# Mixer B, products of keys and queries of a chunk: from two row halves with 128 stationary columns to four quarter positions with 64

## The chip, the cores and the metric

The kernel runs on one core of a Trainium2 chip. The metric is device time in microseconds (us) of one execution, and less is better. Shown are three runs of the kernel before, and one profiled execution. The engines are called as in the profile: PE (TensorE, matmuls), PEld (its loads of the stationary operand, which overlap the matmuls), DVE (VectorE), ACT (ScalarE), POOL (GpSimd) and SP (SyncE, which issues most transfers).

## The reference, cut to what matters

One inference step of a backbone of two layers over 128 context tokens and 1024 latent tokens. The change lies in mixer B of the first layer, an RWKV-7 recurrence with 8 heads of 64, run forward and backward over the tokens:

```python
def step(S, inp):
    r_t, w_t, kk_t, a_t, k_t, v_t = inp
    sa = jnp.einsum('bhvk,bhk->bhv', S, -kk_t)
    S = (S * w_t[:, :, None, :] + sa[..., None] * (kk_t * a_t)[:, :, None, :]
         + v_t[..., None] * k_t[:, :, None, :])
    return S, jnp.einsum('bhvk,bhk->bhv', S, r_t)
```

The kernel computes it by chunks of 64 tokens. Inside a chunk the steps become products: each of the two kinds of keys of the chunk (`k`, and `kk * a`) with each of the two kinds of queries (`kk` and `r`), all of them scaled by the decay. These are four 64x64 tables for each chunk, head and direction. They are masked to a triangle, the `kk` part is inverted by substitution, and a short serial scan carries the state from chunk to chunk.

## The kernel before, in words

The program has four parts one after the other: the input projection and mixer A, mixer B, the output projection of layer one, and all of layer two. Tokens lie in tiles of 128; matmuls are in float32 or in a split float32r.

Mixer B works through nine items. Eight of them are a pair of heads with half of the latent tokens, the ninth takes the context tokens of all four pairs. An item holds, for each direction `d`, four tiles `x` of 128 tokens, each of two chunks `a` of 64. On the partitions lie the two heads of the pair, head `h` on partitions 64h to 64h+63 (`half_of(h)`).

For each item these generators run, and `timeline` mixes those of different items by a table of start and end times (`TIMES`); a scheduler then sets the final order on each engine from priorities and dependences:

- `b_prep` makes the scaled keys `kbt` (four slots of 64 tokens for each tile: of the first chunk the `k` keys and the `kk*a` keys, then those of the second chunk) and the scaled queries `zr` (DVE and ACT, with matmuls L949).
- `b_front` transposes keys, values and queries (L1024, copied out by ACT at L1025 to L1027), then forms the tables in `pa` (L1034). One group of L1034 is two tiles, both chunks and both heads. DVE masks `pa` into `za` (L1040) and `q` (L1042). L1049 makes a first correction of the values from `za`.
- `b_subst` and `b_invert` invert (POOL at L1067 to L1083, then PE at L1108, L1115, L1129 and L1143).
- `b_scan` carries the state: L1186, a DVE addition L1188, L1190, a DVE addition L1197, a scaling on ACT L1199; L1203 and L1163 make the outputs. It is a serial chain of eight steps for each item.
- `b_finish` normalises and gates (L1223 to L1253).

PE also works at the modulation of later layers (L298) in this part.

Every matmul of this part has float32 operands, and each appears in the trace as two records with a weight load each. The array can be used by halves: the partitions of the operands choose the rows of the array, the partitions of the output choose the columns. At L1034 before, the stationary operand is `kbt[s, x, 2a:2a+2]`, 64 partitions by 128 columns (both kinds of keys), and the moving one 64 partitions by 128 columns (both kinds of queries). So a matmul takes one half of the rows and all columns; the two heads take the two halves in turn. L1129 (`b_invert`) already uses a quarter at a time, in this order of rows and columns:

```python
for h, e in ((0, 0), (1, 1), (0, 1), (1, 0)):
    PE.matmul(pe[half_of(h), e, d, x], it.zn[half_of(e), d, x, half_of(h)],
              Rt[half_of(e), 8 * d + 2 * x + h], start=True, stop=True)
```

L1143 takes only two of the four quarters in turn, (0, 0) and (1, 1), and L1049 takes (0, 1) and (1, 0). In the trace a shape like "64*128 64x128" means a stationary operand of 64 partitions by 128 columns and a moving one of 64 by 128.

Of the kernel before, what the change touches and what calls it, by code (L numbers as in the profile page):

```python
# [141 lines left out]
def hybrid_step(ctx: ExitStack, tc: tile.TileContext, I, O, stop=99):  # L142
    nc = tc.nc
    PE, VE, AE, GE, SP = nc.tensor, nc.vector, nc.scalar, nc.gpsimd, nc.sync
# [12 lines left out]
    def tl(pool, shape, tag, dt=F32, bufs=None):  # L157
        uid[0] += 1
        kw = {} if bufs is None else {"bufs": bufs}
        return pool.tile(list(shape), dt, tag=tag, name=f"{tag}_{uid[0]}", **kw)  # L160
# [749 lines left out]
    half_of = lambda j: slice(64 * j, 64 * j + 64)  # L910
# [3 lines left out]
    def part_of(it, d):  # L914
        a = 0 if it.nl > 1 else it.start[d] - P
        return slice(a, a + 512)
# [81 lines left out]
    def b_front(it, d, pool, pre, ps_y, ps_a, vmask):  # L998

        r, v, ke, kbt = it.front[d]  # L1000
        if d == 0:
            it.q, it.kb = {}, {}
            it.VU = tl(it.pool, [P, 4, 2, 2, P], "VU")
            it.zn, it.av = tl(pre, [P, 2, 4, P], "zn", bufs=2), tl(pre, [P, 2, 4, P], "av", bufs=2)
            it.za = tl(pre, [P, 2, 2, 4, 2, 64], "za", bufs=2)
            it.kbs = tl(dp, [2, P, 512 if it.nl > 1 else 1024], "kbs", bufs=2) if it.first else it.prev.kbs
        it.q[d] = tl(it.pool, [P, 8, 2, 64], f"q{d}")
        it.kb[d] = tl(it.pool, [P, 8, P], f"kb{d}")
        order = lambda x: it.chunks(x, d)
        zr = it.zr[d]  # L1010
        kd = hb(pool, [P, 512])
        for i, p in enumerate(it.pairs):
            w = slice(None) if it.nl == 1 else slice(i, i + 1)
            VE.scalar_tensor_tensor(order(kd)[:, w], four(ke)[:, w], rkh[:, p:p + 1], order(r)[:, w], op0=ALU.mult,
                                    op1=ALU.mult)
        SP.dma_start(it.kbs[d][:, part_of(it, d)], kd)
        yield
        for x0 in (0, 2):
            for x in (x0, x0 + 1):
                pn = tl(ps_y, [P, 4, P], "py")  # L1020
                for i, src in enumerate((kbt[:, x, 0:2].rearrange("p a t -> p (a t)"),
                                         kbt[:, x, 2:4].rearrange("p a t -> p (a t)"), v[:, P * x:P * x + P],
                                         zr[:, x, 0].rearrange("p a t -> p (a t)"))):
                    PE.transpose(pn[:, i], src, ident)  # L1024
                AE.copy(it.kb[d][:, 2 * x:2 * x + 2], pn[:, 0:2])  # L1025
                AE.copy(it.VU[:, x, d], pn[:, 2:3].to_broadcast([P, 2, P]))
                AE.copy(it.zn[:, d, x], pn[:, 3])  # L1027
                yield
            pa = tl(ps_a, [P, 2, 2, 2, 2, 64], "pa")
            for x in (x0, x0 + 1):  # L1030
                for a in range(2):
                    for h in range(2):
                        s = half_of(h)
                        PE.matmul(pa[:, h, x - x0, a], kbt[s, x, 2 * a:2 * a + 2].rearrange("p a t -> p (a t)"),  # L1034
                                  zr[s, x, :, 1 - a], start=True, stop=True)
            yield
            mk = lambda i, n: vmask[:, 64 * i:64 * i + 64].rearrange("p (a b m) -> p a b m", a=1, b=1).to_broadcast(
                [P, 2, n, 64])
            for a in range(2):
                VE.tensor_tensor(it.za[:, a, d, x0:x0 + 2].rearrange("p x h t -> p h x t"), pa[:, :, :, a, 0], mk(0, 2),  # L1040
                                 ALU.mult)
            it.tail = VE.tensor_tensor(it.q[d][:, 2 * x0:2 * x0 + 4].rearrange("p c h t -> p h c t"),  # L1042
                             pa.rearrange("p h x a z t -> p h (x a) z t")[:, :, :, 1], mk(1, 4), ALU.mult)
            yield
        pv = tl(ps_y, [P, 4, 2, 64], "py")
        for x in range(4):
            for h in range(2):
                for a in range(2):
                    PE.matmul(pv[half_of(1 - a), x, h], it.za[half_of(a), a, d, x, h],  # L1049
                              it.VU[half_of(a), x, d, a, half_of(h)], start=True, stop=True)  # L1050
        AE.copy(it.av[:, d], pv.rearrange("p x h v -> p x (h v)"))
        yield
# [219 lines left out]
    with ExitStack() as ph2:  # L1272
# [28 lines left out]
        for p in range(4):  # L1301
            a = Item([p], (P, P + 512), last=False)
# [27 lines left out]
        def front(i, d):  # L1330
            return b_front(items[i], d, pool, pre, ps_y, ps_a, ma) if i < len(items) else None
# [37 lines left out]
        for i in range(-2, len(items)):  # L1369
# [47 lines left out]
            t = TIMES[min(i + 2, 2) if i < 5 else 3]  # L1417
# [470 lines left out]
```

## Time and profile before

| | before |
|---|---|
| three runs | 2088.42, 2087.62, 2074.43 us; median 2087.62 |
| profiled execution | a span of 2077.4 us from the first to the last instruction; the page gives no time outside the span, and the median of the runs is 10.2 us more |
| busy over the span | PE 1952.1 us (94%), PEld 1777.4 (86%), DVE 1488.3 (72%), ACT 1058.8 (51%), POOL 673.6 (32%) |
| L1034 | 576 records between 557.9 and 942.1 us |
| the items' front and scan stage | about 557 to 960 us of the span |

A matmul record has its start and a modelled end: records overlap, and the busy time of a group holds the fill of the array as well as its stream. What a run of matmuls takes of PE is therefore read from starts: from a group's first start to its last (its length in the timeline less the length of one record), and from there to the next group's start. The view of waits gives to each idle stretch of an engine what ended it.

### The profile page before, as it was taken

To read this page: it belongs to the slowest core of one execution; us is meant where nothing else is said; L and a number is where in the kernel's file an instruction comes from. 1 tells how busy PE (TensorE), PEld (TensorE's weight loads), DVE (VectorE), ACT (ScalarE), POOL (GpSimd) and SP (SyncE) were. 2 spreads that over 40 slices of the span, in tenths; PEclk is the share of its full clock that TensorE was granted. 3 is DMA by queue.
4 is the path that set the end of the run, shared out by engine and by line. 5 is a ranking of instruction groups with operands and counts; after the bars stand their busy time and mean duration, and the time that the engine had idled before them with its cause. 6 is when DMAs were issued, how large, how long until landed. Compare 5 with 4: busy or idle time off the path is not lost. (4 is left out here: it accounts for less than half of the span.)

```text
span 2077.4 us, 40804 instructions
## 1 busy us (share of the span) xinstructions
PE 1952.1 (94%) x15148; PEld 1777.4 (86%) x15148; DVE 1488.3 (72%) x3821; ACT 1058.8 (51%) x2808; POOL 673.6 (32%) x951
## 2 busy tenths in 40 slices
PE   7899999999789999999989999999999999999998
PEld 7899999999678888777768888999998989898786
DVE  5355567565767787877488587878787878787867
ACT  4343345333446555564356554565555555555643
POOL 0222232332167657575043223121312121212204
PEclk9999999999999999999999999999999999999999
DMA  7511133112555454534576401010101010101325
GB/s 290 163 62 65 61 98 115 63 57 78 181 178 158 146 171 148 157 111 129 167 228 218 133 21 45 15 50 10 51 9 55 6 56 5 55 5 49 106 68 177
DMA packets 165079, 205.72 MB, mean 99 GB/s; under 512 B 16368, under 2 KB 108048, under 8 KB 164880
## 3 DMA queue, kind: packets, MB, share of 16 engines
q1 hardware_dynamic: 162016, 198.25, 30.1%
q10 hardware_dynamic: 2864, 4.85, 0.7%
q8 instruction: 120, 1.97, 0.4%
q14 instruction: 79, 0.65, 0.1%
HBM read 152.32 MB, written 50.74 MB: 98 GB/s over the span
## 5 line engine op out<-in xcount | busy, mean ns | idle before, releaser
L1562 ACT ACTIVATE p<-s,mx 128x384 f32<-128x384 f32 (+1 forms) x400 | 225.1, 572 | 123.0 <-DVE mx L1559 100.3
L1557 DVE TENSOR_REDUCE mc<-s 128x1 f32<-128x384 f32 x384 | 204.4, 551 | 29.3 <-PE s L1555 26.2
L1555 PE MATMUL s<-kst,qs 128*128 128x384 f32 x768 | 196.0, 355 | 14.1 <-ACT p L1562 13.6
L360 PE MATMUL ps<-wch,hh 128*128 128x384 f32 x576 | 205.5, 358 | 3.0 <-DMA raw<-in_wgc_dram 0.9
L361 PE MATMUL ps<-wcl,hh 128*128 128x384 f32 x576 | 198.6, 345 | 4.1 <-POOL wcl L271 4.1
L362 PE MATMUL ps<-wch,hl 128*128 128x384 f32 x576 | 196.4, 341 | 0.3 <-DVE hl L1707 0.2
L407 POOL TENSOR_TENSOR q<-ropea,ropeb 128x256 f32<-128x256 f32 x56 | 44.0, 786 | 442.4 <-DVE ropeb L404 302.3
L374 PE MATMUL ps<-hh,wgh 128*128 128x384 f32 x504 | 174.5, 346 | 5.8 <-DVE bo L242 4.3
L376 PE MATMUL ps<-hh,wgl 128*128 128x384 f32 x504 | 172.4, 342 | 0.0
L375 PE MATMUL ps<-hl,wgh 128*128 128x384 f32 x504 | 171.9, 341 | 0.0
L1555 PEld LDWEIGHTS s<-kst,qs 128*128 128x128 f32 x768 | 127.5, 190 | 29.8 <-ACT p L1562 22.4
L271 POOL TENSOR_TENSOR wgl<-raw,wgh 128x1024 fp32r<-128x1024 f32 (+1 forms) x39 | 75.5, 1939 | 234.5 <-ACT wgh L270 234.5
L1083 POOL TENSOR_TENSOR rp<-rp,tmp 128x126 f32<-128x126 f32 (+22 forms) x279 | 130.3, 467 | 21.9
L1081 POOL TENSOR_TENSOR tmp<-mp,rp 128x126 f32<-128x126 f32 (+22 forms) x279 | 117.8, 422 | 52.3 <-DVE mp L1072 31.1
L1438 ACT CAST ah<-pt 128x512 fp32r<-128x512 f32 (+2 forms) x168 | 86.1, 533 | 79.7 <-PE pt L1593 76.3
L1439 DVE TENSOR_TENSOR al<-pt,ah 128x512 fp32r<-128x512 f32 (+2 forms) x168 | 100.6, 615 | 32.1 <-ACT ah L1438 30.8
L360 PEld LDWEIGHTS ps<-wch,hh 128*128 128x128 f32 x576 | 109.6, 191 | 6.5 <-DVE vl L1439 2.4
L361 PEld LDWEIGHTS ps<-wcl,hh 128*128 128x128 f32 x576 | 109.8, 191 | 6.2 <-POOL wcl L271 5.8
L362 PEld LDWEIGHTS ps<-wch,hl 128*128 128x128 f32 x576 | 109.5, 190 | 1.4 <-DVE hl L1707 1.3
L271 POOL TENSOR_TENSOR wcl<-raw,wch 128x512 fp32r<-128x512 f32 x54 | 76.5, 1423 | 84.5 <-ACT wch L270 84.5
L374 PEld LDWEIGHTS ps<-hh,wgh 128*128 128x128 f32 x504 | 95.4, 189 | 8.1 <-DVE bo L242 4.9
L1575 DVE SCALAR_TENSOR_TENSOR p<-p,lr,p 128x1152 f32<-128x1152 f32 (+1 forms) x72 | 98.4, 1367 | 0.4
(463 smaller groups left out, 5721.7 us busy)
## 6 DMA issues: line engine op xcount, KB each, us to landing
hb<-pbT SPq DMA_DIRECT2D x90, 256.0 KB, 3.9
adaw<-in_ada_w_dram SPq DMA_DIRECT2D x56, 256.0 KB, 3.6
raw<-in_wc_dram SPq DMA_DIRECT2D x48, 256.0 KB, 2.7
adaw<-in_ada_w_dram SPq DMA_DIRECT2D x8, 1024.0 KB, 10.9
pbT<-bm SPq DMA_DIRECT2D x16, 512.0 KB, 2.7
low<-lowT SPq DMA_DIRECT2D x16, 512.0 KB, 4.1
raw<-in_wo_dram SPq DMA_DIRECT2D x32, 256.0 KB, 2.8
raw<-in_wpb_dram SPq DMA_DIRECT2D x13, 512.0 KB, 3.4
```

The costliest lines, as they stand in the source:

```text
L271: eng.tensor_tensor(lo[:, j:j + w], raw[:, :w], hi[:, j:j + w].bitcast(F32), ALU.subtract)
L360: PE.matmul(ps[:, :n], hh[:, k, s], wh[:, k], start=k == 0, stop=False)
L361: PE.matmul(ps[:, :n], hh[:, k, s], wl[:, k], start=False, stop=False)
L362: PE.matmul(ps[:, :n], hl[:, k, s], wh[:, k], start=False, stop=k == KT - 1)
L374: PE.matmul(ps[:, :THIRD], wh[:, k], hh[:, k, s], start=k == 0, stop=False)
L375: PE.matmul(ps[:, :THIRD], wh[:, k], hl[:, k, s], start=False, stop=False)
L376: PE.matmul(ps[:, :THIRD], wl[:, k], hh[:, k, s], start=False, stop=k == KT - 1)
L1081: eng.tensor_tensor(tv, m[:, j - a:j - a + 1, 0:j].to_broadcast([P, n, j]), rpb[:, t:16, j:j + 1].to_broadcast([P, n, j]), ALU.mult)
L1083: eng.tensor_tensor(rpb[:, t:16, 0:j], rpb[:, t:16, 0:j], tv, ALU.add)
L1555: PE.matmul(s[c][:, :w], qs[:, e, z], hd.kp[:, z] if own else hd.kst[:, z, w * c:w * c + w], start=e == 0, stop=e == 1)
L1557: VE.tensor_reduce(mc[:, c:c + 1] if nb > 1 else mx, s[c][:, :w], axis=AX.X, op=ALU.min)
L1562: AE.activation(e[:, w * c:w * c + w], s[c][:, :w], AF.Exp, scale=-1.0, bias=mx, accum_out=sums[:, z, c:c + 1])
```

## The change

In `b_front`, the 128 stationary columns of each product are cut into two halves `e` of 64, one for each kind of keys. Half `e` goes to the columns whose outputs are partitions 64e to 64e+63 of `pa`, where the same numbers stood before. There are now four matmuls for each tile and chunk in place of two, in the order (0,0), (1,1), (0,1), (1,0) of head and half. The moving operand stays 64 by 128, and is now streamed once for each half. What is written to `pa`, and all that reads it, is the same.

```diff
@@ -1029,10 +1029,10 @@
             pa = tl(ps_a, [P, 2, 2, 2, 2, 64], "pa")
             for x in (x0, x0 + 1):
                 for a in range(2):
-                    for h in range(2):
+                    for h, e in ((0, 0), (1, 1), (0, 1), (1, 0)):
                         s = half_of(h)
-                        PE.matmul(pa[:, h, x - x0, a], kbt[s, x, 2 * a:2 * a + 2].rearrange("p a t -> p (a t)"),
-                                  zr[s, x, :, 1 - a], start=True, stop=True)
+                        PE.matmul(pa[half_of(e), h, x - x0, a], kbt[s, x, 2 * a + e], zr[s, x, :, 1 - a],
+                                  start=True, stop=True)
             yield
```

In the whole program 288 matmuls of L1034 become 576. The scheduler's order moves a little with it, only in the mixer B part; POOL's order is unchanged. On PE the 288 matmuls stood in 53 unbroken runs, 26 of them whole groups of eight; the 576 stand in 58 runs, 25 of them whole groups of sixteen.

The first place is on PE, in an item whose scan (L1186, L1190, L1203) is mixed with the products of a later item. `pa` is the table, `zr` and `kbt` are queries and keys, `sc` and `yb` belong to the scan. Before:

```order
L949 MATMUL py_6804<-low_6791,lora_6793 128x512 x2
L1034 MATMUL pa_6818<-zr_1211_6637,kbt_6640 128x128 x2
L1186 MATMUL sc_6763<-G_991_5695,E_6646 128x128 x2
L1034 MATMUL pa_6818<-zr_1211_6637,kbt_6640 128x128 x2
L1203 MATMUL yb_6727<-zr_1009_5745,S_995_5699 128x64
L1034 MATMUL pa_6818<-zr_1211_6637,kbt_6640 128x128
L1190 MATMUL sc_6763<-VU_5813,kb_1032_5819 128x128
L1190 MATMUL sc_6763<-VU_5813,kb_1046_5911 128x128
L1203 MATMUL yb_6727<-zr_1035_5831,S_995_5699 128x64
L1034 MATMUL pa_6818<-zr_1211_6637,kbt_6640 128x128 x3
```

The same place in the changed kernel:

```order
L1034 MATMUL pa_6882<-zr_1211_6701,kbt_6704 64x128
L1190 MATMUL sc_6792<-VU_5813,kb_1032_5819 128x128
L1190 MATMUL sc_6792<-VU_5813,kb_1046_5927 128x128
L949 MATMUL py_6868<-low_6855,lora_6857 128x512 x2
L1034 MATMUL pa_6882<-zr_1211_6701,kbt_6704 64x128 x4
L1186 MATMUL sc_6827<-G_991_5695,E_6710 128x128 x2
L1034 MATMUL pa_6882<-zr_1211_6701,kbt_6704 64x128 x4
L1203 MATMUL yb_6791<-zr_1009_5745,S_995_5699 128x64
L1203 MATMUL yb_6791<-zr_1035_5831,S_995_5699 128x64
L1190 MATMUL sc_6827<-VU_5813,kb_1032_5819 128x128
L1190 MATMUL sc_6827<-VU_5813,kb_1046_5927 128x128
L1034 MATMUL pa_6882<-zr_1211_6701,kbt_6704 64x128 x7
```

The group of eight stood in runs of 2, 2, 1 and 3 and now stands in runs of 1, 4, 4 and 7 of sixteen; one run starts ahead of the scan's L1190, and the two L1203 stand together.

The second place is on DVE, in one of two items where the same rows change places: the scan's additions L1188 (`VU`) and L1197 (`G`) among the work for later items (L1014) and for the output of an earlier one (L1226). Before:

```order
L1042 TENSOR_TENSOR q_1469_8140<-pa_8252,cstones_5690 128x2x4x64
L990 TENSOR_TENSOR kbt_8249<-hb_8265,hb_8191 128x4x2x64
L1188 TENSOR_TENSOR VU_6753<-VU_6753,sc_8294 64x2x128
L1014 SCALAR_TENSOR_TENSOR hb_8367<-hb_8265,rkh_5649,hb_8181 128x512
L1226 TENSOR_TENSOR hb_8270<-hb_8270,hb_8271 128x512
L1197 TENSOR_TENSOR G_992_5696<-S_993_5697,sc_8294 64x2x64 x2
L307 TENSOR_SCALAR gs_5_69<-py_8285,prm_60 128x2
```

The same place in the changed kernel:

```order
L1042 TENSOR_TENSOR q_1469_8268<-pa_8388,cstones_5690 128x2x4x64
L990 TENSOR_TENSOR kbt_8385<-hb_8409,hb_8319 128x4x2x64
L1014 SCALAR_TENSOR_TENSOR hb_8511<-hb_8409,rkh_5649,hb_8309 128x512
L1226 TENSOR_TENSOR hb_8414<-hb_8414,hb_8415 128x512
L1188 TENSOR_TENSOR VU_6817<-VU_6817,sc_8438 64x2x128
L307 TENSOR_SCALAR gs_5_69<-py_8429,prm_60 128x2
L1197 TENSOR_TENSOR G_992_5696<-S_993_5697,sc_8438 64x2x64 x2
```

L1188 moved behind L1014 and L1226, and L1197 behind L307.

## Prediction

> **What bounds the kernel now.** I read the page first, for the engine that is busy most, then busy times of the stretch in which L1034 runs, then the groups of PE in that stretch.
>
> ```profile
> span 2077.4 us, 40804 instructions
> PE 1952.1 (94%) x15148; PEld 1777.4 (86%) x15148; DVE 1488.3 (72%) x3821; ACT 1058.8 (51%) x2808; POOL 673.6 (32%) x951
> ```
>
> PE is busy 94% of the span. The stretch of the change is 557 to 960 us, here as the sum of five equal parts of it (403 us), with the columns of the view's own head:
>
> ```profile
> core 0: us, PE busy (x) PEld busy (x) DVE busy (x) ACT busy (x) POOL busy (x), PEclk, DMA share, GB/s
> sum 403.00, PE 363.25 PEld 314.20 DVE 309.41 ACT 226.81 POOL 256.11; mean PE 72.65 PEld 62.84 DVE 61.88 ACT 45.36 POOL 51.22
> ```
>
> PE is at 363 of 403 us (90%), DVE at 309 (77%). So PE, in its fixed order, is the nearest thing to a bound, and I count what L1034 takes of PE as lying on the path. The groups of PE in this stretch (busy us, mean ns of one, idle before):
>
> ```profile
> L298 PE MATMUL py<-prm,adaw 128*128 128x128 f32 x442 | 64.5, 295 | 1.8 <-DMA adaw<-in_ada_w_dram 1.6
> L1034 PE MATMUL pa<-zr,kbt 64*128 64x128 f32 x576 | 49.6, 296 | 2.3 <-DVE q L1042 1.5 <-DVE kbt L990 0.8
> L1190 PE MATMUL sc<-VU,kb 128*128 128x128 f32 x224 | 37.6, 290 | 8.8 <-DVE VU L1188 8.6
> ```
>
> L1034 covers 49.6 us, 2.4% of the span. To make the kernel faster by 1% (21 us) the change would have to take away over two fifths of that. The scan's L1190 waits 8.6 us for L1188; who waits on L1034's side is this:
>
> ```profile
> PEld pa L1034 <- issue: 8.9, 26, 1.7
> DVE za L1040 <- PE pa L1034: 10.0, 7, 3.9
> ```
>
> The chain that ended last is no help here: as the profile shows it, it reaches back only some tens of us from the end, into layer two.
>
> **What a group of L1034 costs.** A record has one length (min, median, max in ns):
>
> ```profile
> L1034 PE MATMUL pa<-zr,kbt x576: 271/272/579, 557.9 to 942.1; 64*128 64x128 f32 x192
> L1129 PE MATMUL pa<-Rt,zn x576: 218/218/312, 623.0 to 1035.6; 64*64 64x64 f32 x192
> L1143 PE MATMUL sc<-av,Rt x576: 218/218/332, 623.2 to 1037.5; 64*64 64x64 f32 x192
> ```
>
> Length of a group less one record is the time from its first to its last start. Whole and broken groups in the timeline (start, length):
>
> ```profile
> 605.45 0.27 PE L1024 MATMUL py<-cst,zr 128*128 128x128 f32 x1
> 605.65 1.16 PE L1034 MATMUL pa<-zr,kbt 64*128 64x128 f32 x16
> 606.80 1.02 PE L298 MATMUL py<-prm,adaw 128*128 128x128 f32 x7
> ...
> 629.74 0.49 PE L1034 MATMUL pa<-zr,kbt 64*128 64x128 f32 x4
> 630.16 0.71 PE L1186 MATMUL sc<-G,E 128*128 128x128 f32 x4
> ...
> 633.04 0.71 PE L1034 MATMUL pa<-zr,kbt 64*128 64x128 f32 x6
> 633.68 0.44 PE L1024 MATMUL py<-cst,kbt 128*128 128x128 f32 x2
> ...
> 636.32 0.48 PE L1034 MATMUL pa<-zr,kbt 64*128 64x128 f32 x2
> ```
>
> One product (x2): 0.48 - 0.27 = 0.21 us from its first record to its second. Two (x4): 0.22. So the two row halves run side by side. Three (x6): 0.44, as four would, since the odd one takes its rounds alone. Eight (x16): 0.89. Each further pair of products costs (0.89 - 0.22) / 3 = 0.223 us, two rounds of 0.1115. A round is the time in which every position in use starts one record. The first round is longer by 0.10: the first load of 128 columns has nothing to hide it. Entering from a 128-row matmul takes 605.65 - 605.45 = 0.20 and leaving 630.16 - (629.74 + 0.22) = 0.20; from one such matmul to the next it is 0.11.
>
> **What four positions cost.** The changed kernel's form is not in this trace, 64 columns with 128 moving. Its two neighbours are, with 64 moving columns: L1129 in four positions, L1143 in two.
>
> ```profile
> 1034.70 1.16 PE L1129 MATMUL pa<-Rt,zn 64*64 64x64 f32 x64
> 1035.69 2.03 PE L1143 MATMUL sc<-av,Rt 64*64 64x64 f32 x64
> ...
> 708.80 0.33 PE L1129 MATMUL pa<-Rt,zn 64*64 64x64 f32 x2
> ```
>
> L1143 makes 64 records in 32 rounds: (2.03 - 0.22) / 31 = 0.058 a round. L1129 makes them in 16 rounds: 1.16 - 0.22 = 0.94, which is 0.11 for the first (from the x2 row, 0.33 - 0.22) and 0.83 / 14 = 0.059 for each after it. So going from two to four positions left the round as it was. And 0.1115 is nearly twice 0.058, as 128 moving columns are twice 64. Forecast for the new form: a round of 0.1115 with four positions, and a first round of 0.11 + 0.05 = 0.16, with half the load of before. Four starts are some 0.02 apart in all (64 records of L1129: 0.94 - 0.11 - 14 x 0.058 = 0.02).
>
> There are 36 groups (9 items, 2 directions, 2 halves). A whole group before is 8 products in 2 positions, 8 rounds. After, it is 16 products in 4 positions: 8 rounds again. **The array was full before**, two halves by 128 columns; it is full after, four quarters. Twice the records at twice the rate is the same time.
>
> **The sum.** In PE's order there are 53 runs of L1034 before. Two products share two rounds, an odd one takes them alone: 151 pairs of rounds, 53 of them first ones. 53 x 0.22 + 98 x 0.223 = 33.5 us from first to last starts. After, 58 runs and four products to two rounds: 155 pairs, 58 x 0.18 + 97 x 0.223 = 32.1 us. That saves 1.4 us, all of it from the shorter first load. But five more runs each cost an entering and a leaving, less the step they take the place of: 5 x (0.20 + 0.20 - 0.11) = 1.5 us. Net: +0.1 us, so nothing.
>
> Bounds: if all five extra runs stand where PE would have waited anyway, -1.4. If the shorter load shows nowhere (each load covered by the drain of what went before), +1.5. The 576 further instructions of each kind (load and matmul) are no price of their own: L1129 starts 64 records in 0.94 us, twice as dense as the 32 in 0.85 that the forecast comes to for a whole group.
>
> Here a rule bears on the joins. L1034 at 572.46 follows L1049, a 64x64 form:
>
> ```profile
> 571.85 0.68 PE L1049 MATMUL py<-VU,za 64*64 64x64 f32 x16
> 572.46 1.16 PE L1034 MATMUL pa<-zr,kbt 64*128 64x128 f32 x16
> 573.55 0.50 PE L949 MATMUL py<-low,lora 128*128 128x512 f32 x1
> ```
>
> L1049's last start is 571.85 + 0.68 - 0.22 = 572.31, so the join took 0.15; L1129 to L1143 above, both 64x64, took 1035.69 - (1034.70 + 0.94) = 0.05. The Trainium skill, "TensorEngine Tiling (Array Packing)", Key Properties, says that changing the tiling mode drains the engine, while changing the tile alone does not. The trace agrees: 0.10 us at a change of form. By that rule L1034 and L1049 would join without a drain after the change. PE's order has six such joins (two enterings, four leavings): -0.6 us in the sum, by an estimate from these rows.
>
> **What the new order moves.** DVE gets the scan's L1188 later, behind two operations, in two items; their length:
>
> ```profile
> L1014 DVE SCALAR_TENSOR_TENSOR hb<-hb,rkh,hb x24: 335/740/1202, 557.3 to 934.1; 128x512 f32<-128x512 f32 x16, 128x128 f32<-128x128 f32 x8
> L1226 DVE TENSOR_TENSOR hb<-hb,hb x9: 677/684/876, 731.4 to 1030.1; 128x512 f32<-128x512 f32 x9
> ```
>
> That is 0.74 + 0.68 = 1.42 us, and L1190 queued behind it on PE waits (the 8.6 us above). Twice: +2.8 us at worst, nothing where DVE waited there for L1186. Other moves go the other way (the scan's L1203 no longer split around L1190). I take 0 and -3 to +3. No transfer moves but one pair of rows on SP's queue, and POOL's order is unchanged, so I give them nothing.
>
> Total: 2077.4 + 0 in the span, and with the 10.2 us by which the median of the runs stands above this span, 2087.6; I say 2087. The mechanism has bounds of -5 to +5 (loads and joins -2, +1.5; order -3, +3). The three runs of before lie 14 us apart (2074.4 to 2088.4, 0.7%), more than the whole effect. A change under 1% cannot be told from none here.
>
> **Rivals.**
>
> Four positions don't run side by side with 128 moving columns. The two halves `e` of one head stream the same queries separately; if these two took turns, a round of four would be two rounds: 8 x 0.1115 = 0.89 us more for each of the 36 groups, +32 us, 2119. It decides for "slower" from +21 us, a round of 0.184. For it: no row has four positions with 128 moving. Against it: L1129's 0.059, where column halves of the same rows also run at once. Chance 4%. A milder form: the Trainium skill, "TensorE: Matmul & The Clock Gate", Measured speedup vs the span model, has four tiles of 32 rows with 512 moving columns gain 3.07 times, not 4. By that a round would be 0.1115 x 4 / 3.07 = 0.145 and the sum +9.7 us (36 groups of 8 rounds), 2097, an estimate; L1129 beside L1143 shows no such loss from two to four.
>
> The order is what counts: L1188 and L1190 later in several items, +3 to +10 us, 2090 to 2097, or as much earlier. The waits for and against are the ones above, small and many. Chance 14%, within 1%.
>
> The shorter load opens the path: PEld's 8.9 us ahead of L1034, DVE's 10.0 us for `pa`, and 58 x 0.05 = 2.9 us of loads all vanish: -21.8 us, 2066. Against it: PEld's wait is mostly the leaving of the matmul before, and leaving takes 0.20 whatever comes. Chance 3%.
>
> That the change doesn't do what it says (positions not in turn) could be only where runs are broken; the count of 155 pairs of rounds holds that.
>
> **How the numbers follow.** Forecast, within 1% by its own mechanism: 79%; with the order rival, 93% within 1%. Slower by over 1%: 4%. Faster by over 1%: 3%. The range: the lowest run less the mechanism's 5 is 2069; the highest run plus 5, and half of the milder form, is 2098.
>
> **What would show it.** L1034 with 1152 records of 64*64 64x128; a whole group (x32) 0.84 to 0.86 us from first to last start, four starts nearly at once and a round of 0.11; leaving at 0.20. Against me: a round of 0.15 or more; a whole group of 0.6 or less; DVE's wait for `pa` far from 10 us; a stretch 557 to 960 that ends over 5 us elsewhere.

## The result and the profile after

| | before | changed |
|---|---|---|
| median of the executions | 2084.93 us of 6 (2074.43 to 2088.42) | 2092.85 us of 6 (2091.91 to 2099.15) |
| changed over before | | 1.0058, 95% interval 1.0036 to 1.0080 |
| profiled execution, span | 2077.4 us | 2091.4 us (its own time 2093.23 us) |
| mean granted clock over the span | 0.984 | 0.974 |

The change makes the kernel slower by 0.58%. That is inside the range of the forecast and under the 1% named in it, but the interval excludes no change, and the forecast was no change. A repeat on another chip (below) gave the same.

The head of the page of the changed kernel, the span and the busy time of each engine:

```profile
span 2091.4 us, 41942 instructions
PE 1964.6 (94%) x15724; PEld 1786.9 (85%) x15724; DVE 1490.9 (71%) x3821; ACT 1057.8 (51%) x2808; POOL 670.6 (32%) x951
```

PE is busy 94% as before, but for 12.5 us more (1964.6 against 1952.1). The obvious suspect is L1034. The rows of that line, in the changed kernel's view of one line (the record's shortest, median and longest time in ns, first and last start, form; and below it who waits for it and what its load waits for):

```profile
L1034 PE MATMUL pa<-zr,kbt x1152: 269/269/473, 559.6 to 957.1; 64*64 64x128 f32 x192
...
  issue: 10.1, 29
...
  DVE za L1040: 10.6, 7
```

There are 1152 records, as forecast. DVE waits 10.6 us for `pa` (10.0 before), and the load waits 10.1 us (8.9 before). Neither moved by more than 1.2 us. The timeline of a part of a group and of a whole one (start, length):

```profile
601.17 0.45 PE L1034 MATMUL pa<-zr,kbt 64*64 64x128 f32 x8
...
607.57 0.27 PE L1024 MATMUL py<-cst,zr 128*128 128x128 f32 x1
607.77 1.10 PE L1034 MATMUL pa<-zr,kbt 64*64 64x128 f32 x32
608.80 1.16 PE L298 MATMUL py<-prm,adaw 128*128 128x128 f32 x8
```

First to last start takes 1.10 - 0.269 = 0.83 us, where the old form took 0.89. Entering took 607.77 - 607.57 = 0.20, and leaving 608.80 - (607.77 + 0.83) = 0.20. The run of eight records, two rounds, takes 0.45 - 0.27 = 0.18, so the six further rounds of a whole group take (0.83 - 0.18) / 6 = 0.11 each. The groups of PE in the stretch of the change, here 557 to 970 us (busy us, mean ns of one, idle before):

```profile
L298 PE MATMUL py<-prm,adaw 128*128 128x128 f32 x448 | 69.8, 309 | 2.8 <-DMA adaw<-in_ada_w_dram 2.8
L1034 PE MATMUL pa<-zr,kbt 64*64 64x128 f32 x1152 | 50.8, 294 | 2.7 <-DVE q L1042 1.6 <-DVE kbt L990 1.1
L1190 PE MATMUL sc<-VU,kb 128*128 128x128 f32 x224 | 38.1, 294 | 9.0 <-DVE VU L1188 8.8
```

L1034 covers 50.8 us in place of 49.6. But L298, which the change doesn't touch, went from a mean of 295 to 309 ns a record. A reason stands in the column of the granted clock. The stretch of the change before, by parts (window, length, busy time with instructions of PE, PEld, DVE, ACT and POOL, granted clock, DMA share, GB/s); first part, fourth, and the sum:

```profile
557.00:640.00 83.00, 70.23 (x830) 59.59 (x829) 58.86 (x124) 41.30 (x112) 50.81 (x107) 0.92 0.61 184
...
800.00:880.00 80.00, 72.07 (x1122) 62.59 (x1123) 65.94 (x157) 45.10 (x113) 48.29 (x102) 1.00 0.52 160
```

And in the changed kernel:

```profile
557.00:640.00 83.00, 70.36 (x919) 58.96 (x917) 53.20 (x113) 37.19 (x98) 48.02 (x106) 0.83 0.59 180
...
800.00:880.00 80.00, 74.55 (x1206) 64.80 (x1196) 63.40 (x153) 45.83 (x112) 44.28 (x101) 0.94 0.52 160
...
sum 403.00, PE 365.57 PEld 313.10 DVE 301.18 ACT 218.89 POOL 240.31; mean PE 73.11 PEld 62.62 DVE 60.24 ACT 43.78 POOL 48.06
```

PE is busy as long as before in the same 403 us (365.6 against 363.3), while DVE, whose work is the same, got through 301.2 us of it in place of 309.4. So the kernel is behind by 960 us with PE no less busy: part of PE's time ran at a lower clock. The stage from the first L1042 to L1707 (output projection) took 534.9 us, and 522.7 before: 12.2 of the span's 14.0 us are there.

Between two profiles the clock differs by chance too, so from here on times of several executions decide.

### The profile page after: what moved, and what is told of

It reads as the page before. It is cut to its first block, busy times and chain, and to the rows that moved or that the text cites. A ratio compares the mean times of both kernels' runs of the same rounds, so it can differ in the third digit from the quotient of the medians.

```text
span 2091.4 us, 41942 instructions
## 1 busy us (share of the span) xinstructions
PE 1964.6 (94%) x15724; PEld 1786.9 (85%) x15724; DVE 1490.9 (71%) x3821; ACT 1057.8 (51%) x2808; POOL 670.6 (32%) x951
## 5 line engine op out<-in xcount | busy, mean ns | idle before, releaser
L1439 DVE TENSOR_TENSOR al<-pt,ah 128x512 fp32r<-128x512 f32 (+2 forms) x168 | 100.6, 615 | 36.8 <-ACT ah L1438 35.5
## 6 DMA issues: line engine op xcount, KB each, us to landing
adaw<-in_ada_w_dram SPq DMA_DIRECT2D x8, 1024.0 KB, 10.6
```

## The experiments

The edit has two effects. The form of L1034 is one; the other is the scheduler's order, which moves as a consequence. Theory A: the form costs, by something that single groups don't show. Theory B: the order costs. To part them, an order is written out as a list, and each engine's instructions are chained to it by dependences that add no wait; the arithmetic stays.

### The form alone, and the order alone

The new form with each engine in the order of the kernel before (the list is left out here):

```diff
--- after.py
+++ new form, old order
+def keep_order(tc, nc):
+    seqs = json.loads(zlib.decompress(base64.b85decode(ORDER)))
+    ...
+            if prev is not None:
+                tc.add_manual_dep(i, prev.name, mybir.DependencyInfo(
+                    mybir.DependencyClass.NoSync, mybir.DependencyReason.DATA), reason="order")
+            prev = i
...
+        keep_order(tc, nc)
```

> The products of L1034 in the new form (64 stationary columns, four positions), while every engine keeps the order of the kernel before: each old product of 128 columns is replaced where it stands by its two halves. Order theory (the new order of the instructions costs the 0.6%, the form nothing): ratio to before 0.998 to 1.002, half-clock time of PE near the 67 us of before. Form theory (quarter positions count as less activity, so TensorE's granted clock falls more often): ratio 1.005 to 1.008, half-clock time near 109 us. If both share it: 1.002 to 1.005.

The old form in the changed kernel's order; each old product stands where the second of its two halves stood. The edit is the same function with another list, on the kernel before:

> The products of L1034 in the old form (128 stationary columns, two row halves), while every engine keeps the order of the changed kernel: each pair of halves is replaced, at the place of the second, by the old product. Order theory: ratio to before 1.004 to 1.008, half-clock time near 109 us. Form theory: 0.998 to 1.002, near 67 us.

And the changed kernel once more beside these two:

> The changed kernel itself, beside the two others on the same chip: 1.004 to 1.008 by either theory. If it comes out within 0.002 of before, the 0.6% was the chance of that chip or of the phase in which the clock's windows fell.

Measured on one chip, with the kernel before at a median of 2083.59 us there:

| | median, us | over before, 95% interval |
|---|---|---|
| new form, old order | 2083.82 | 1.0001 [0.9987, 1.0015] |
| old form, new order | 2091.64 | 1.0044 [1.0028, 1.0061] |
| both, the changed kernel | 2097.64 | 1.0063 [1.0047, 1.0079] |

**The form alone costs nothing that shows, the order costs it.** The 1152 records of the new form, in the old order, run in the old time. Theory A falls. The changed kernel stands 0.2% above the old form in the same order; the two intervals overlap, so whether the form costs something in that order is not settled.

The second sign, PE's time at half clock (a granted clock of 0.5), is less clear. In the profiled executions it was 83 us with the new form in the old order and 91 us with the old form in the new order. Both lie between the 67 us of before and the 109 us of the changed kernel, and one execution of each doesn't decide; the means further down do more.

One thing that moves with the order is the waits of the scan. L1197 is DVE's addition to the state behind L1190 on PE, 136 of them between 557 and 1090 us, a serial chain. Its rows give busy time, mean ns, and DVE's idle time before it. Before:

```profile
L1197 DVE TENSOR_TENSOR G<-S,sc 64x128 f32<-64x128 f32 x136 | 38.6, 284 | 30.4 <-PE sc L1190 19.6 <-PE py L1024 2.6 <-ACT hb L956 2.0
```

New form, old order:

```profile
L1197 DVE TENSOR_TENSOR G<-S,sc 64x128 f32<-64x128 f32 x136 | 38.6, 284 | 31.1 <-PE sc L1190 20.5 <-PE py L1024 2.6 <-ACT hb L956 2.0
```

Old form, new order:

```profile
L1197 DVE TENSOR_TENSOR G<-S,sc 64x128 f32<-64x128 f32 x136 | 38.6, 284 | 33.5 <-PE sc L1190 22.7 <-PE py L1024 2.6 <-ACT hb L956 2.0
```

The changed kernel:

```profile
L1197 DVE TENSOR_TENSOR G<-S,sc 64x128 f32<-64x128 f32 x136 | 38.7, 284 | 34.7 <-PE sc L1190 24.7 <-PE py L1024 2.6 <-ACT hb L956 2.0
```

With the old order DVE waits 19.6 and 20.5 us for L1190, with the new one 22.7 and 24.7 (25.3 in the repeat of the changed kernel). The step after it in the chain, the scaling on ACT, waits for L1197 longer too. In the waits of the kernel before, and then of the changed one, between 557 and 1090 us (total, times, longest):

```profile
ACT S L1199 <- DVE G L1197: 30.1, 26, 2.3
```

```profile
ACT S L1199 <- DVE G L1197: 35.6, 30, 3.4
```

In the new form with the old order that wait was 31.6 us, in the old form with the new order 35.5. So with the new order the state of the scan is handed on later, by 2 to 5 us in all at this step. Some of it is PE's lower clock and not other work ahead of L1190; the profile doesn't part the two, and that these waits are what makes the kernel longer is not shown.

### Is it one place?

If one place carried it, half of the new order would cost all and the other half nothing. Two more lists, both with the new form: the new order up to about 660 us (the first 500 instructions of the part's block on PE, 200 on DVE and on ACT, 250 on SP) with the old order after it, and the reverse.

```diff
--- new form, old order
+++ new form, new order in one part
-ORDER = (before's order)
+ORDER = (the changed kernel's up to the cut, before's after it; or the reverse)
```

> New form of L1034. On every engine the order of the changed kernel up to about 660 us of the span (the differences around the inversion and the first scan steps of the first item), and from there on the order of the kernel before. In the profiles the changed kernel was 7 us behind before by 650 us and 15 us behind by 950 us. If each part of the new order costs by itself: ratio to before 1.002 to 1.004. If the first part alone is the cause and the rest follows from it (a clock that is late stays late): 1.005 to 1.007. If only the later part costs: 0.999 to 1.001.

> The complement: new form of L1034, the order of before on every engine up to about 660 us, and the order of the changed kernel after that. Each part by itself: 1.002 to 1.004. First part alone the cause: 0.999 to 1.001. Later part alone: 1.005 to 1.007.

Is it this order, or any other order than the old? Two versions of the kernel before, old form, no list; the scheduler is only given slightly other times for `b_front` in `TIMES`, 0.02 less or 0.02 more in each of its four rows:

```diff
--- before.py
+++ times less
-            ((0.17, 1.0), (0.38, 1.09), (-0.04, 0.46), (0.11, 0.32), (0.05, 0.3), ...
+            ((0.17, 1.0), (0.38, 1.09), (-0.04, 0.46), (0.09, 0.3), (0.05, 0.3), ...
...
+++ times more
+            ((0.17, 1.0), (0.38, 1.09), (-0.04, 0.46), (0.13, 0.34), (0.05, 0.3), ...
```

> The kernel before, old form, with one number of the mixing table moved in each row: the first direction's front starts and ends 0.02 of an item earlier. The scheduler answers with a reordering about as large as that of the change (185 rows of difference on PE, against some 200 for the change without the rows of L1034 itself). If any reordering of this size costs, because the old order was the best found: ratio 1.002 to 1.006. If it was this order that was poor: 0.998 to 1.002.

> The same with the first direction's front 0.02 of an item later. The same two expectations: any reordering costs, 1.002 to 1.006; only the change's order was poor, 0.998 to 1.002.

PE's order differs from before's in 185 rows with the smaller times, about as many as with the change. Measured on one chip, with the kernel before at a median of 2081.31 us there; beside it what DVE waits for L1190 ahead of L1197, as in the rows above:

| | median, us | over before, 95% interval | DVE's wait for L1190, us |
|---|---|---|---|
| new order in the first part only | 2090.65 | 1.0052 [1.0033, 1.0072] | 22.4 |
| new order in the later part only | 2093.47 | 1.0062 [1.0043, 1.0082] | 24.9 |
| old form, times 0.02 less | 2093.61 | 1.0062 [1.0046, 1.0078] | 27.0 |
| old form, times 0.02 more | 2089.58 | 1.0047 [1.0026, 1.0069] | 21.3 |

By the medians each half of the new order costs about as much as the whole: 0.52% + 0.62% would be 1.14%, and the whole costs 0.58 to 0.63%. None of the expectations fits both halves: 0.2 to 0.4% each if each costs by itself, 0.5 to 0.7% of one and nothing of the other if one part is the cause. The profiled executions say otherwise. The stage from the first L1042 to L1707 took 525.1 us with the new form in the old order, 531.2 and 530.5 with a half of the new order, 534.9 and 539.0 with all of it: there the halves do add. The rest of what these two kernels lost had come before: they reached the first L1042 2.3 and 3.6 us later than the new form in the old order, in a part of the program whose order is the same in all. So whether the costs add stays open.

Two small moves of the old kernel's times, with no change of form at all, cost as much (expected 0.2 to 0.6% if any other order costs, none if only the change's order was poor). **Each of the five other orders is 0.44 to 0.63% slower than the old one**; two of the five are half the old one. So it is not that the new order is an especially bad one: among the orders timed here the old one is the good one, and the edit loses it. Why it is (numbers in `TIMES` that were picked by measuring would do it) was not tried.

The longest wait of that kind belongs to the times 0.02 less, 27.0 us. The smallest, 21.3 with the times 0.02 more, is hardly above the 20.5 of the old order with the new form. So the scan's wait goes with the order but doesn't account for the time in each case.

### The clock

The mean granted clock over all timed executions, and their mean time:

| | executions | mean clock | mean us | excess at equal clock, us |
|---|---|---|---|---|
| before | 29 | 0.979 | 2082.9 | |
| new form, old order | 11 | 0.979 | 2083.7 | 1.1 |
| old form, new order | 6 | 0.977 | 2092.1 | 6.4 |
| changed, both chips | 12 | 0.974 | 2095.4 | 6.1 |
| new order, first part | 6 | 0.977 | 2091.4 | 4.4 |
| new order, later part | 6 | 0.975 | 2093.9 | 6.5 |
| times less | 6 | 0.976 | 2093.4 | 7.3 |
| times more | 7 | 0.974 | 2090.9 | 2.2 |

The last column compares each execution with those of before at the same clock (to the third digit), where there are any. Within each kernel, too, a lower clock means a longer time: 1.13 us (standard error 0.10) for each 0.001 over all executions. So for the changed kernel 0.979 - 0.974 = 0.005 makes some 5.6 us of the 12.5, and at equal clock 6.1 remain. Only 6 of its 12 executions have a partner at the same clock; with one slope for all executions the excess is 6.8 us for the changed kernel (standard error 1.0), 1.1 (0.8) for the new form in the old order and 2.7 (1.1) for the times 0.02 more. About half of the changed kernel's loss goes with the clock, with the times 0.02 more about two thirds, and the rest is there without it. This is a correlation: a longer time and a lower clock may both come from the same stalls, and no run held the clock up with the new order.

In the profiled executions, the stage from the first L1042 to L1707 shows where PE's time went (one execution of each, not all on one chip; idle is the stage less PE's busy time):

| | stage, us | PE idle, us | at half clock, us |
|---|---|---|---|
| before | 522.7 | 47.5 | 23.9 |
| new form, old order | 525.1 | 47.2 | 41.0 |
| old form, new order | 537.8 | 51.6 | 46.9 |
| changed | 534.9 | 47.4 | 55.9 |
| changed, repeat | 539.0 | 46.5 | 68.3 |
| new order, first part | 531.2 | 50.3 | 44.1 |
| new order, later part | 530.5 | 45.2 | 54.2 |
| times less | 537.0 | 48.1 | 45.5 |
| times more | 532.8 | 40.9 | 65.2 |

In the changed kernel PE waits no longer than before; its busy time grew, at a lower clock. With the old form in the new order the waits grew too. The half-clock time by itself doesn't give the stage: with the new form in the old order it is 17 us more than before, and the stage 2.4 us longer.

How a stall lowers the clock shows in single places. In the changed kernel, L298 waits for its weights (timeline, start and length; the idle time before it and its cause at the end):

```profile
617.79 0.90 PE L1049 MATMUL py<-VU,za 64*64 64x64 f32 x16
620.34 0.46 PE L298 MATMUL py<-prm,adaw 128*128 128x128 f32 x2 [1.65 <-DMA adaw<-in_ada_w_dram]
620.73 1.20 PE L1108 MATMUL sc<-hb,za 32*32 32x32 f32 x64
621.86 1.90 PE L298 MATMUL py<-prm,adaw 128*128 128x128 f32 x8
```

The same eight records of L298 after L1108 took 1.16 us in the kernel before (at 618.71 us); here they take 1.90. The stretches around this place, same columns as above:

```profile
616.90:620.32 3.42, 1.79 (x36) 1.46 (x36) 3.33 (x7) 2.63 (x6) 2.35 (x4) 1.00 1.03 310
620.32:622.08 1.76, 1.74 (x68) 1.60 (x69) 1.65 (x2) 0.99 (x3) 0.13 (x2) 1.00 0.57 155
622.08:632.32 10.24, 10.24 (x180) 9.00 (x180) 5.65 (x11) 2.24 (x4) 8.83 (x19) 0.50 0.41 132
632.32:635.73 3.41, 3.34 (x48) 2.59 (x44) 0.73 (x3) 3.12 (x8) 2.86 (x8) 1.00 0.41 153
```

PE is busy for 1.79 of 3.42 us, and 1.76 us later the granted clock is 0.50 for 10.24 us (three times 3.41). At half speed that is the work of about five us; by the eight records above (1.16 us for 1.90) of about six. So a stall of 1.65 us costs 4 to 5 us more in this place, by an estimate from these rows. Over all nine profiled executions PE's busy share tells when this happens. Cut at the clock's own steps of 3.413 us, there are 109 steps at full clock with PE busy for under 1.7 us, and half clock follows on 103 of them; on the 4812 with PE busy for 2.56 us or more it follows 9 times. Here the step is 618.67 to 622.08 us, with PE busy for 1.76 us; between the two bounds it goes either way. So where a stall falls among the steps matters too, and not its length alone. This one isn't the order's doing: in the new form with the old order the same wait was 1.97 us, and halved the clock as well, while in the profile of before PE waited there only 1.31 us, for DVE, and the clock stayed. In the later-part kernel, which has the old order there, the clock of 557 to 640 us was 0.82. So the clock of a single place is partly chance, and only the means of the table bear on the order.

## Why the prediction was right or wrong

- **What a group of L1034 costs, and what four positions cost: right.** The group takes 0.83 us from first to last start (forecast 0.84 to 0.86), a further round 0.11, entering and leaving 0.20. The array was full before, and twice the records at twice the rate is the same time. The rivals with positions that take turns (+32 us, +9.7 us) fall by it.
- **The sum: right in its result.** "Net: +0.1 us, so nothing": the form alone measured 1.0001 [0.9987, 1.0015], from -2.7 to +3.1 us. That run keeps the old 53 runs of L1034, so it bears on the shorter first load (-1.4 us) alone; the five extra runs (+1.5 us) came only with the new order and were not timed by themselves.
- **The joins with L1049: half right.** The rows of the changed kernel:

```profile
576.44 0.91 PE L1049 MATMUL py<-VU,za 64*64 64x64 f32 x16
577.27 1.10 PE L1034 MATMUL pa<-zr,kbt 64*64 64x128 f32 x32
...
705.00 1.10 PE L1034 MATMUL pa<-zr,kbt 64*64 64x128 f32 x32
705.94 0.63 PE L1049 MATMUL py<-VU,za 64*64 64x64 f32 x16
```

  Leaving to L1049 takes 705.94 - (705.00 + 0.83) = 0.11 in place of 0.20 to a matmul of 128 rows. Entering from L1049 takes 577.27 - (576.44 + 0.91 - 0.22) = 0.14, and took 0.15 before. So in these rows the 0.10 us that the estimate took off each join came only at the leaving.
- **What the new order moves: wrong, and this is the step that failed.** "I take 0 and -3 to +3." The order alone costs 0.44% [0.28, 0.61], 9 us, and with the form 0.58 to 0.63%. I priced it at the one place where rows change around L1188, as two operations of DVE. PE's wait for L1188 hardly moved: 8.6 us before, 8.8 in the changed kernel, 10.0 with the old form in the new order. What moved is one step further in the chain, DVE's wait for L1190 (19.6 to 24.7 us) and ACT's wait for L1197 (30.1 to 35.6), and PE's time at half clock in the stage (23.9 to 55.9 us). How much of the 9 us each of them makes stays open. I also took it that moves of both signs cancel, without a row that prices them; against an order that is better than all five others timed, none gained.
- **The order as a rival: right in its size, and half right in its mechanism.** "+3 to +10 us, 2090 to 2097" holds the 2092.85, and the order is what counts; but the wait that it names, L1190 behind L1188, is not the one that moved, and it had 14% and "as much earlier" beside it.
- **The range: no credit to the mechanism.** The 2092.85 lies inside 2069 to 2098 because the range starts from the lowest and the highest run of before. The measured change of the medians, +7.9 us, is outside the mechanism's own bounds of -5 to +5.
- **The clock: not in the prediction at all.** I counted stalls at their own length. In the place shown one stall of 1.65 us cost 4 to 5 us more by the estimate above, and in the means half of the loss goes with the clock.
- **The 10.2 us "around" the span: wrong.** The profiled execution of the changed kernel took 2093.23 us with a span of 2091.4, so 1.8 us lie outside. That of before was one of its kernel's shorter ones, about 2079.2 us. The size of the forecast is not hurt, since it used the median; but of the 14.0 us between the two spans some 6 are that chance, since the medians differ by 7.9.
- **What would show it.** The stretch that ends over 5 us elsewhere was named against me, and came: the first L1042 of the changed kernel started 1.5 us later than before, and at 960 us of the span the work was some 15 us late.

## What to carry to other kernels

Splitting a matmul into more array positions gained nothing here, where the positions in use already filled the array: count rows times columns in use before counting instructions. An edit that changes how many instructions a scheduler sees can also change the order, and against an order that happens to be a good one, that alone cost half a per cent here; so time the edit once with the old order held, before judging it. Price a stall of TensorE not by its length alone, since it may be paid again at a lower clock (here 1.65 us of stall, and then 10.24 us at half clock).

## What the runs showed of the hardware that was not expected

- The granted clock fell to half after a stretch of 3.4 us in which PE was busy for 1.79 us, behind one stall of 1.65 us, and stayed there for 10.24 us. The Trainium skill, "TensorE: Matmul & The Clock Gate", What's actually happening, has a window of 3413 ns that runs free of the program: the trace agrees on the length, since the stretch at half clock is three times 3.41 us. The same page, Why this matters for your kernels, asks for no idle gap over some 3 us; here a stall of half that length was followed by the lower clock, so the measurement is the stricter.
- The windows' chance position may be what makes executions of one kernel differ (before: 2076 us at a clock of 0.983, 2091 at 0.973); that was not tried.
